# Modulation steps that end 24 steps before the end of layer 0's FFN, and sums of squares on VectorE from the fifth output tile on

## The chip, the core and the metric

The kernel runs on one core of a Trainium2 chip. TensorE multiplies matrices, VectorE and ScalarE work on rows of 128 partitions, GpSimd does so too, SyncE issues DMAs. Each engine works off its own queue of instructions in program order and waits on semaphores for the others. The metric is the device time of one execution in microseconds, as the median of several runs. All times below are microseconds unless marked ns.

## The reference

Four layers in fp32 on 256 tokens of width 1024. The first two (the "first block") have a token mixer and a swiglu FFN, each between two norms, with gates, scales and shifts that come from a modulation vector; in layer 0 a second stream of 256 context tokens goes through the same weights, so that N is 512 there and 256 in layer 1.

```python
mod  = silu(c)     @ w_mod[l] + b_mod[l]      # 6 vectors of 1024 for each layer
modc = silu(c_ctx) @ w_mod[l] + b_mod[l]      # the same for the context stream
h  = rms_norm(xl, g_pre_mix[l]) * (1.0 + sc1) + sh1
y  = token_mixer(h, ...)
xl = xl + gt1 * rms_norm(y, g_post_mix[l])
h  = rms_norm(xl, g_pre_ffn[l]) * (1.0 + sc2) + sh2
xl = xl + gt2 * rms_norm(swiglu(h, ...), g_post_ffn[l])
...                                           # two hybrid layers, and a final norm
```

The change touches the order of `mod` of layer 1 and the end of layer 0, and the sums that the `rms_norm` of y needs.

## The kernel before

Each fp32 matmul is made as three matmuls on split operands (`mm3`, lines 164 to 166): high by high, high by low, low by high. A weight tile arrives by DMA as `raw`; ScalarE rounds it into `whi` (L154), and VectorE, or for some tiles GpSimd, subtracts to get `wlo` (L155). `whi` and `wlo` have four buffers each, `raw` has two. Activations lie transposed, with the model's 1024 channels in eight tiles of 128 partitions and the tokens along the free dimension.

The order of the work is a list of steps with a cost each, written by the planner code below and issued in that order; every engine's queue follows it, with some steps marked as urgent (`soon`) so that they are moved ahead of others. `merge(main, side)` spreads the steps of `side` among those of `main` in proportion to cost, so that both lists end together.

In layer 0's FFN the main list `fs` has 100 steps: gate and up projections and down-projection in two halves of the hidden width. At its end the down-projection's output tiles m=4 to 7 run by halves of the tokens: first half, `y_rms` of the first half and eight `join` tiles (residual, norm, next layer's input), with the second half's tiles between. L1179 adds the two hidden halves on VectorE. The side list `ms` has 71 steps: modulation groups made on VectorE (`mod_v`: L476 and L478, on 512-column `mraw` tiles of w_mod, four parts per group), each group closed by a flush (L484 on TensorE sums over partitions, L489 on VectorE adds the bias).

`y_add` takes an output tile m: ScalarE scales by the gate (`z`, L580), then three sums are built up over m = 0 to 7: the square of y (L596, ScalarE), z*x (L598, VectorE) and the square of z (L599, ScalarE). Tile 0 starts the accumulators `acc`, tile 7 is kept apart as `last`, and L594 adds tiles 1 to 6 in, on GpSimd, only m=6 on VectorE. `y_rms` lets TensorE sum over partitions: L611 reads `acc`, L612 reads `last`; VectorE reads the result (L614, L617), computes the root (lines 269 to 279), TensorE spreads it over the partitions (L316), and VectorE and GpSimd apply it (L645, L646). The next norm makes the input of the next matmuls, tile by tile: L558 on VectorE, L560 on ScalarE, L561 on VectorE.

`y_add` with three sums runs in mixer 0, FFN 0 and mixer 1, and with one sum in FFN 1; where N is 512 the last tiles and `y_rms` go by token halves.

Of the kernel before, what the change touches and what calls it, by code (L numbers as in the profile page):

```python
# [10 lines left out]
ALU = mybir.AluOpType  # L11
# [34 lines left out]
class Kern:  # L46
# [523 lines left out]
    def y_add(self, m, ps, tok, full):  # L570


        nc, V = self.nc, self.v
        t0, t1 = tok
        z = V["z", m]
        G = V["G"]
        x = self.xs[m]
        for s in range(t0 // 256, t1 // 256):
            c = slice(256 * s, 256 * s + 256)
            nc.scalar.activation(z[:, c], ps[:, c], AF.Copy, scale=G[:, m, s:s + 1])  # L580
        c = slice(t0, t1)

        def put(i, f):
            if m == 0:
                V["acc", i] = self.slot()
                f(V["acc", i])
                return
            t = self.slot()
            f(t)
            if m == 7:  # L590
                V["last", i] = t
                return
            a = V["acc", i][:, c]
            (nc.vector if m == 6 else nc.gpsimd).tensor_tensor(a, a, t[:, c], op=ALU.add)  # L594

        put(0, lambda o: nc.scalar.activation(o[:, c], ps[:, c], AF.Square))  # L596
        if full:
            put(1, lambda o: nc.vector.tensor_tensor(o[:, c], z[:, c], x[:, c], op=ALU.mult))  # L598
            put(2, lambda o: nc.scalar.activation(o[:, c], z[:, c], AF.Square))  # L599
# [485 lines left out]
    def block1(self):  # L1085
        nc, a = self.nc, self.a
# [39 lines left out]
        def join(l, N, t0, s_scale, s_shift, gain, hot):  # L1126

            def tile_(i):
                if i == 0:
                    V["pre"] = pre(l, N, t0, s_scale, s_shift, gain)  # L1130
                V["pre"](i, V["rb"][:, 256:], t0 + 256)
            return [H(lambda: self.y_rms(t0, True))] + [X(self.soon(lambda i=i: tile_(i), AHEAD if hot else 0))
                                                        for i in range(8)]

        H = lambda f, c=0.5: ("x", c, self.soon(f))
        for l in range(2):
            N = 512 if l == 0 else 256
            if l == 0:
                fs = [self.mod(0, g) for g in (2, 3, 0, 1)]
                st.append(X(fs[0]))  # L1140
                st.append(X(x_in))
                st += [X(f) for f in fs[1:]]
                st.append(H(pre0))
                st.append(X(self.setup_rest))

            def begin(l, s_gate, gain):
                V["G"] = self.post_cols(l, s_gate, self.par[gain, l])
                for m in range(8):
                    V["z", m] = None

            def y_evac(m, ps, tok):
                if V["z", m] is None:
                    V["z", m] = self.slot()
                self.y_add(m, ps, tok, True)

            jm = lambda t0, hot, l=l, N=N: join(l, N, t0, 4, 3, "g_pre_ffn", hot)
            mix = self.mixer1(l, lambda: self.h, N, y_evac, jm(0, False) if l == 0 else None)
            at = next(i for i in range(len(mix)) if mix[i][0] == "begin")
            mix[at] = X(lambda l=l: begin(l, 2, "g_post_mix"))
            if l == 1:  # L1160
                mix = merge(mix[:8], jf(256, False), 1) + mix[8:]
            P_ = lambda p: st.append(X(lambda: setattr(self, "phase", p), 0))
            P_(2 * l)
            st += mix
            P_(2 * l + 1)
            if l == 1:
                st += self.mem_kv(0)
            st += jm(256 if l == 0 else 0, True)

            def f_evac(m, ps, tok, h, nh, l=l, N=N):  # L1170
                c = slice(*tok)
                if h < nh - 1:
                    V["y", m] = self.slot()
                    nc.scalar.activation(V["y", m][:, c], ps[:, c], AF.Copy)
                    return
                src = ps
                if nh > 1:
                    src = V["y", m]
                    nc.vector.tensor_tensor(src[:, c], src[:, c], ps[:, c], op=ALU.add)  # L1179
                if V["z", m] is None:  # L1180
                    V["z", m] = self.slot()
                self.y_add(m, src, tok, l == 0)

            fs = []
            jf = lambda t0, hot: join(1, 512, t0, 1, 0, "g_pre_mix", hot)
            self.ffn(fs, a["w_ffn_in"][l], a["w_ffn_out"][l], lambda: self.h, N, f_evac,
                     mid=jf(0, False) if l == 0 else None)
            if l == 0:
                ms = []
                self.mod_v(ms, 0, (10, 11), 2)  # L1190
                ms.append(X(lambda: begin(0, 5, "g_post_ffn")))
                self.mod_v(ms, 1, (2, 3, 0, 1), 2)
                self.mod_v(ms, 1, (4, 5, 8, 9, 6, 7, 10, 11), 1)
                fs = merge(fs, ms)
            else:
                fs = merge(fs, [X(self.tables), X(lambda: self.mem_norm(1)), X(lambda: begin(1, 5, "g_post_ffn"))])
            st += fs
            if l == 1:
                st += self.mem_kv(1)
            if l == 1:  # L1200
                def last():
                    self.y_rms(0, False)
                    self.next_h("l0_norm_mix_2")

                    for i in range(8):
                        self.residual(i, 0)
                        self.x_split(i)
                        self.sq_add("x", self.xs[i][:, :256], 256, i, 8)
                st.append(H(last))
# [579 lines left out]
def merge(main, side, now=0):  # L1789

    if now:
        return side[:now] + merge(main, side[now:])
    tot = sum(e[1] for e in main) or 1.0
    ts = sum(max(e[1], 0.05) for e in side) or 1.0
    out = []
    at, done, j = 0.0, 0.0, 0
    for e in main:
        while j < len(side) and done / ts <= at / tot and at > 0:
            out.append(side[j])
            done += max(side[j][1], 0.05)  # L1800
            j += 1
        out.append(e)
        at += e[1]
    return out + side[j:]
# [114 lines left out]
```

## Time and profile before

| quantity | value |
|---|---|
| runs | 2310.51, 2314.38, 2311.95 us; median 2311.95 |
| the profiled execution's own time | 2310.39 us |
| its span | 2308.5 us |
| TensorE busy | 2175.2 us (94%) |
| VectorE busy | 1622.4 us (70%) |
| ScalarE busy | 1085.5 us (47%) |
| GpSimd busy | 535.8 us (23%) |
| L594 on GpSimd | 68 instructions, 70.7 us busy |
| L478 on VectorE | 224 instructions, 174.2 us busy |
| DMA | 319.18 MB, mean 138 GB/s |

The span is the time from the first to the last instruction in the profile; the time of the execution contains it and a little around it. Shares of busy time are averages over stages that differ: TensorE is full in most of the kernel, and waits where one stage ends and the next begins. In the profile PE is TensorE, DVE is VectorE, ACT is ScalarE, POOL is GpSimd; L594 is line 594 of the kernel before. PEclk is the TensorE clock that was granted, as a share of 2.4 GHz.

### The profile page before, as it was taken

To read this page: it belongs to the slowest core of one execution; us is meant where nothing else is said; L and a number is where in the kernel's file an instruction comes from. 1 tells how busy PE (TensorE), PEld (TensorE's weight loads), DVE (VectorE), ACT (ScalarE), POOL (GpSimd) and SP (SyncE) were. 2 spreads that over 40 slices of the span, in tenths; PEclk is the share of its full clock that TensorE was granted. 3 is DMA by queue.
4 is the path that set the end of the run, shared out by engine and by line. 5 is a ranking of instruction groups with operands and counts; after the bars stand their busy time and mean duration, and the time that the engine had idled before them with its cause. 6 is when DMAs were issued, how large, how long until landed. Compare 5 with 4: busy or idle time off the path is not lost.

```text
span 2308.5 us, 37343 instructions
## 1 busy us (share of the span) xinstructions
PE 2175.2 (94%) x14512; PEld 1974.4 (86%) x14512; DVE 1622.4 (70%) x3227; ACT 1085.5 (47%) x2098; POOL 535.8 (23%) x545
## 2 busy tenths in 40 slices
PE   4999999999989999989999999999988999999998
PEld 3777777788888888878888899899976999998998
DVE  5677787959678745577977976775575766676665
ACT  5345665332333222233566555554546544466443
POOL 1354443320340111142333312100343100110000
PEclk8999999999999999998999999999997999999999
DMA  8321112435414555553322455465541555543553
GB/s 276 94 74 55 56 56 74 147 114 173 155 65 155 162 193 165 166 162 115 128 74 74 147 168 184 133 201 172 166 108 58 165 183 174 191 161 100 185 182 120
DMA packets 296625, 319.18 MB, mean 138 GB/s; under 512 B 20544, under 2 KB 264352, under 8 KB 296448
## 3 DMA queue, kind: packets, MB, share of 16 engines
q1 hardware_dynamic: 293072, 311.27, 41.9%
q0 software_dynamic: 2224, 3.43, 0.6%
q8 instruction: 114, 1.87, 0.3%
q10 hardware_dynamic: 1152, 2.10, 0.3%
q14 instruction: 63, 0.52, 0.1%
HBM read 315.72 MB, written 1.05 MB: 137 GB/s over the span
## 4 chain that ended last, share of the span: by engine, by line
PE 73%; DVE 15%; ACT 4%; issue 3%; POOL 2%; DMA 1%; ACTq 0%; DVEq 0%; POOLq 0%
PE p L164 21%; PE p L165 21%; PE p L166 20%; DVE wlo L155 3%; PE p L743 1%; DVE t L478 1%; DVE t L796 1%; PE tr L883 1%; PE p L247 1%; PE p L249 1%; PE p L248 1%; PE tr L484 1%; DVE b L855 1%; PE tr L1267 1%; POOL t L794 1%
## 5 line engine op out<-in xcount | busy, mean ns | idle before, releaser
L164 PE MATMUL p<-t,whi 128*128 128x256 f32 (+1 forms) x3724 | 1176.3, 320 | 10.8 <-ACT t L560 6.5
L166 PE MATMUL p<-t,wlo 128*128 128x256 f32 (+1 forms) x3724 | 1177.4, 317 | 8.9 <-POOL wlo L155 4.7
L165 PE MATMUL p<-t,whi 128*128 128x256 f32 (+1 forms) x3724 | 1179.7, 318 | 3.7 <-DVE t L261 1.7
L164 PEld LDWEIGHTS p<-t,whi 128*128 128x128 f32 x3724 | 716.2, 194 | 60.8 <-ACT t L560 7.8
L166 PEld LDWEIGHTS p<-t,wlo 128*128 128x128 f32 x3724 | 721.1, 194 | 53.5 <-DVE wlo L155 5.5
L165 PEld LDWEIGHTS p<-t,whi 128*128 128x128 f32 x3724 | 722.0, 194 | 47.7 <-DVE t L261 2.5
L154 ACT ACTIVATE whi<-raw 128x1024 fp32r<-128x1024 f32 (+4 forms) x487 | 491.1, 1019 | 502.2 <-PE p L165 302.2
L155 DVE TENSOR_TENSOR wlo<-raw,whi 128x1024 fp32r<-128x1024 f32 (+4 forms) x443 | 549.6, 1242 | 197.0 <-PE p L166 88.3
L155 POOL TENSOR_TENSOR wlo<-raw,whi 128x1024 fp32r<-128x1024 f32 (+2 forms) x44 | 102.9, 2339 | 501.6 <-ACT whi L154 445.1
L478 DVE SCALAR_TENSOR_TENSOR t<-mraw,big,t 128x512 f32<-128x512 f32 x224 | 174.2, 817 | 19.3 <-DMA mraw<-in_w_mod_dram 17.9
L794 POOL TENSOR_TENSOR t<-t,t 128x512 f32<-128x512 f32 (+1 forms) x120 | 136.2, 1135 | 193.3 <-ACT t L793 191.1
L260 ACT ACTIVATE t<-t 128x256 fp32r<-128x256 f32 (+1 forms) x115 | 54.4, 474 | 156.3 <-DVE t L689 112.1
L594 POOL TENSOR_TENSOR t<-t,t 128x256 f32<-128x256 f32 (+1 forms) x68 | 70.7, 1068 | 244.2 <-ACT t L596 240.0
L299 POOL TENSOR_TENSOR t<-t,t 128x256 f32<-128x256 f32 (+1 forms) x27 | 27.1, 1003 | 414.1 <-ACT t L297 403.1
L247 PE MATMUL p<-whi,t 128*128 128x256 f32 x352 | 102.6, 291 | 2.7 <-ACT t L858 2.7
L796 DVE SCALAR_TENSOR_TENSOR t<-u,big,t 128x512 f32<-128x512 f32 (+1 forms) x120 | 102.2, 851 | 0.8
L743 PE MATMUL p<-t,t 64*128 64x256 f32 (+2 forms) x528 | 77.6, 377 | 25.7 <-DVE t L261 11.7
L249 PE MATMUL p<-whi,t 128*128 128x256 f32 x352 | 99.9, 284 | 0.0
L248 PE MATMUL p<-wlo,t 128*128 128x256 f32 x352 | 99.8, 284 | 0.0
L689 DVE TENSOR_TENSOR t<-t,p 128x256 f32<-128x256 f32 (+1 forms) x91 | 43.2, 475 | 78.9 <-PE p L166 78.9
L743 PEld LDWEIGHTS p<-t,t 64*128 64x128 f32 x528 | 50.6, 210 | 46.9 <-issue 18.3
L257 ACT ACTIVATE t<-p 128x256 fp32r<-128x256 f32 x72 | 27.7, 384 | 123.0 <-DVE p L726 98.5
(298 smaller groups left out, 2532.1 us busy)
## 6 DMA issues: line engine op xcount, KB each, us to landing
raw<-in_w_in_dram SPq DMA_DIRECT2D x60, 1024.0 KB, 5.1
raw<-in_l_w_gate_up_dram SPq DMA_DIRECT2D x44, 1024.0 KB, 5.1
raw<-in_w_ffn_in_dram SPq DMA_DIRECT2D x42, 1024.0 KB, 5.2
mraw<-in_w_mod_dram SPq DMA_DIRECT2D x80, 512.0 KB, 4.2
raw<-in_l_w_in_dram SPq DMA_DIRECT2D x15, 1024.0 KB, 5.1
raw<-in_l_w_down_dram SPq DMA_DIRECT2D x16, 896.0 KB, 4.8
t<-in_w_mod_dram SPq DMA_DIRECT2D x32, 256.0 KB, 5.4
raw<-in_w_attn_out_dram SPq DMA_DIRECT2D x8, 1024.0 KB, 5.2
```

The lines of the kernel that those rows point to most:

```text
L154: nc.scalar.activation(p.hi, src, AF.Copy)
L155: eng.tensor_tensor(p.lo, src, p.hi, op=ALU.subtract)
L164: mm(ps, lh, rh, start=first, stop=False)
L165: mm(ps, lh, rl, start=False, stop=False)
L166: mm(ps, ll, rh, start=False, stop=last)
L247: mm(ps[:, :256], lh, p.hi[:, k % 4], start=k == 0, stop=False)
L248: mm(ps[:, :256], lh, p.lo[:, k % 4], start=False, stop=False)
L249: mm(ps[:, :256], ll, p.hi[:, k % 4], start=False, stop=k == 7)
L478: nc.vector.scalar_tensor_tensor(acc, w[:, k], c, acc, op0=ALU.mult, op1=ALU.add)
L743: self.nc.tensor.matmul(out[half], q[i // 2][h, qs], k[i % 2][h, ks], start=i == 0, stop=i == 2)
L794: nc.gpsimd.tensor_tensor(acc, acc, t, op=ALU.add)
L796: i = nc.vector.scalar_tensor_tensor(acc, u, w, acc, op0=ALU.mult, op1=ALU.add)
```

## The change

Two places are edited. In `y_add` the adds of tiles 4 and 5 go to VectorE, as that of tile 6 did. In layer 0 the modulation list is merged with the FFN's steps except the last 24, which follow without any modulation between them. Those 24 are the last seven down-projection steps of the first token half (m=5 to 7), `y_rms` of the first token half, the second halves and the eight `join` tiles.

```diff
@@ -591,7 +591,7 @@
             a = V["acc", i][:, c]
-            (nc.vector if m == 6 else nc.gpsimd).tensor_tensor(a, a, t[:, c], op=ALU.add)
+            (nc.vector if m >= 4 else nc.gpsimd).tensor_tensor(a, a, t[:, c], op=ALU.add)
@@ -1191,7 +1191,9 @@
                 self.mod_v(ms, 1, (2, 3, 0, 1), 2)
                 self.mod_v(ms, 1, (4, 5, 8, 9, 6, 7, 10, 11), 1)
-                fs = merge(fs, ms)
+
+                n = len(fs) - 24
+                fs = merge(fs[:n], ms) + fs[n:]
```

VectorE's queue in FFN 0 around the output tiles m=2 and 3, before (the L598 of m=2 reads t85, that of m=3 t87; x2 is two instructions in a row):

```order
L478 SCALAR_TENSOR_TENSOR t1526_8529<-mraw1533_8579,big_70,t1526_8529 128x512 x2
L155 TENSOR_TENSOR wlo1531_8557<-raw_657,whi1530_8556 128x768
L478 SCALAR_TENSOR_TENSOR t1526_8529<-mraw1540_8615,big_70,t1526_8529 128x512 x2
L478 SCALAR_TENSOR_TENSOR t1526_8529<-mraw1554_8705,big_70,t1526_8529 128x512
L155 TENSOR_TENSOR wlo1535_8584<-raw_657,whi1534_8583 128x768
L478 SCALAR_TENSOR_TENSOR t1526_8529<-mraw1554_8705,big_70,t1526_8529 128x512
L1179 TENSOR_TENSOR t1318_7282<-t1318_7282,p1529_8536 128x512
L598 TENSOR_TENSOR t1538_8609<-t1536_8603,t85_292 128x512
L1179 TENSOR_TENSOR t1322_7310<-t1322_7310,p1532_8560 128x512
L155 TENSOR_TENSOR wlo1548_8653<-raw_657,whi1547_8652 128x640
L598 TENSOR_TENSOR t1545_8646<-t1543_8640,t87_299 128x512
```

The same place after the change:

```order
L598 TENSOR_TENSOR t1531_8549<-t1529_8543,t83_285 128x512
L155 TENSOR_TENSOR wlo1539_8588<-raw_657,whi1538_8587 128x768
L155 TENSOR_TENSOR wlo1542_8611<-raw_657,whi1541_8610 128x768
L1179 TENSOR_TENSOR t1321_7305<-t1321_7305,p1536_8563 128x512
L489 TENSOR_TENSOR big_70<-tr1547_8642,big_70 128x4
L598 TENSOR_TENSOR t1545_8636<-t1543_8630,t85_292 128x512
L1179 TENSOR_TENSOR t1325_7333<-t1325_7333,p1540_8591 128x512
L155 TENSOR_TENSOR wlo1556_8686<-raw_657,whi1555_8685 128x640
L598 TENSOR_TENSOR t1553_8679<-t1551_8673,t87_299 128x512
L489 TENSOR_TENSOR big_70<-tr1558_8708,big_70 128x4
```

Six L478 stood ahead of the L1179 of m=2; none stands between the L598 of m=1 (t83) and that of m=3 now.

VectorE's queue where the first token half ends, from the L598 of m=5 (t91) to that of m=6 (t93) and the adds behind it, before:

```order
L598 TENSOR_TENSOR t1565_8766<-t1563_8761,t91_313 128x256
L476 TENSOR_SCALAR t1571_8797<-mraw1570_8795,big_70 128x512
L478 SCALAR_TENSOR_TENSOR t1571_8797<-mraw1570_8795,big_70,t1571_8797 128x512
L478 SCALAR_TENSOR_TENSOR t1571_8797<-mraw1587_8884,big_70,t1571_8797 128x512
L155 TENSOR_TENSOR wlo1573_8802<-raw_657,whi1572_8801 128x768
L478 SCALAR_TENSOR_TENSOR t1571_8797<-mraw1587_8884,big_70,t1571_8797 128x512
L155 TENSOR_TENSOR wlo1576_8825<-raw_657,whi1575_8824 128x768
L1179 TENSOR_TENSOR t1350_7511<-t1350_7511,p1569_8776 128x256
L478 SCALAR_TENSOR_TENSOR t1571_8797<-mraw1621_9038,big_70,t1571_8797 128x512
L598 TENSOR_TENSOR t1579_8849<-t1577_8844,t93_320 128x256
L594 TENSOR_TENSOR t1516_8488<-t1516_8488,t1578_8846 128x256
L594 TENSOR_TENSOR t1517_8490<-t1517_8490,t1579_8849 128x256
```

The same place after:

```order
L598 TENSOR_TENSOR t1572_8795<-t1570_8790,t91_313 128x256
L594 TENSOR_TENSOR t1524_8516<-t1524_8516,t1571_8792 128x256
L594 TENSOR_TENSOR t1525_8518<-t1525_8518,t1572_8795 128x256
L594 TENSOR_TENSOR t1526_8520<-t1526_8520,t1573_8798 128x256
L155 TENSOR_TENSOR wlo1578_8826<-raw_657,whi1577_8825 128x768
L155 TENSOR_TENSOR wlo1581_8849<-raw_657,whi1580_8848 128x768
L1179 TENSOR_TENSOR t1354_7524<-t1354_7524,p1576_8805 128x256
L598 TENSOR_TENSOR t1584_8873<-t1582_8868,t93_320 128x256
L594 TENSOR_TENSOR t1524_8516<-t1524_8516,t1583_8870 128x256
L594 TENSOR_TENSOR t1525_8518<-t1525_8518,t1584_8873 128x256
L594 TENSOR_TENSOR t1526_8520<-t1526_8520,t1585_8876 128x256
L1179 TENSOR_TENSOR t1357_7546<-t1357_7546,p1579_8829 128x256
```

The L476 and four L478 of the last modulation group are gone from here, and three L594 of m=5 have come in; those of m=4 stand just ahead of the rows.

GpSimd's queue there, from the 512-wide adds of m=3 on, before (t1516 to t1518 are the three accumulators; a wlo is a share of a weight tile):

```order
L594 TENSOR_TENSOR t1516_8488<-t1516_8488,t1544_8643 128x512
L594 TENSOR_TENSOR t1517_8490<-t1517_8490,t1545_8646 128x512
L594 TENSOR_TENSOR t1518_8492<-t1518_8492,t1546_8649 128x512
L155 TENSOR_TENSOR wlo1562_8742<-raw_657,whi1561_8741 128x640
L594 TENSOR_TENSOR t1516_8488<-t1516_8488,t1558_8731 128x256
L594 TENSOR_TENSOR t1517_8490<-t1517_8490,t1559_8734 128x256
L594 TENSOR_TENSOR t1518_8492<-t1518_8492,t1560_8737 128x256
L594 TENSOR_TENSOR t1516_8488<-t1516_8488,t1564_8763 128x256
L594 TENSOR_TENSOR t1518_8492<-t1518_8492,t1566_8769 128x256
L594 TENSOR_TENSOR t1517_8490<-t1517_8490,t1565_8766 128x256
L155 TENSOR_TENSOR wlo1582_8857<-raw_657,whi1581_8856 128x640
L155 TENSOR_TENSOR wlo1630_9082<-raw_657,whi1629_9081 128x640
```

After, with t1524 to t1526 as the accumulators:

```order
L594 TENSOR_TENSOR t1524_8516<-t1524_8516,t1552_8676 128x512
L594 TENSOR_TENSOR t1525_8518<-t1525_8518,t1553_8679 128x512
L594 TENSOR_TENSOR t1526_8520<-t1526_8520,t1554_8682 128x512
L155 TENSOR_TENSOR wlo1569_8771<-raw_657,whi1568_8770 128x640
L155 TENSOR_TENSOR wlo1587_8881<-raw_657,whi1586_8880 128x640
L646 TENSOR_TENSOR t83_285<-t83_285,t1529_8543 128x256
```

The six 128x256 adds of m=4 and 5 are gone; those of 512 columns and the wlo behind them stand as they did.

In all, 32 of the 68 adds on GpSimd move to VectorE: 12 in mixer 0, 12 in FFN 0, 6 in mixer 1 and 2 in FFN 1. The rest of the order differs only in layer 0's FFN, where the modulation steps stand closer together, and slightly among the matmuls at the end of mixer 0, whose adds move.

## Rows read from the trace of the kernel before

**Rows 1.** Windows: start and end, length, busy time and instructions per engine, PEclk, DMA.
```profile
690.00:1000.00 310.00, 310.00 (x1502) 261.64 (x1501) 193.88 (x280) 85.75 (x122) 33.83 (x15) 1.00 0.53 168
1020.00:1040.00 20.00, 12.59 (x97) 11.97 (x96) 18.85 (x23) 8.56 (x17) 17.60 (x12) 0.94 0.57 172
1060.00:1113.00 53.00, 46.81 (x331) 45.43 (x330) 44.97 (x121) 23.99 (x46) 19.27 (x28) 0.87 0.37 119
```

**Rows 2.** Waits of TensorE, 1000 to 1060 us: us in total, times, longest.
```profile
PE tr L611 <- DVE t L594: 4.7, 1, 4.7
PE p L166 <- POOL wlo L155: 1.7, 1, 1.7
PE p L166 <- DVE wlo L155: 1.0, 1, 1.0
```

**Rows 3.** Timeline of TensorE: start, us, then idle before and releaser in brackets.
```profile
1039.04 0.58 PE L611 MATMUL tr<-big,t 128*128 128x1 f32 x2 [4.65 <-DVE t L594]
```

**Rows 4.** Timeline of GpSimd, 1016 to 1036 us.
```profile
1016.66 10.22 POOL L594 TENSOR_TENSOR t<-t,t 128x512 f32<-128x512 f32 x6 [4.34 <-ACT t L596]
1026.85 2.11 POOL L155 TENSOR_TENSOR wlo<-raw,whi 128x640 fp32r<-128x640 f32 x1
1028.92 6.63 POOL L594 TENSOR_TENSOR t<-t,t 128x256 f32<-128x256 f32 x6
```

**Rows 5.** Window of the instructions of L478 alone, VectorE.
```profile
1028.00:1056.00 28.00, 7.36 (x7) 0.76 0.47 142
```

**Rows 6.** Timeline of VectorE, 1028 to 1056 us.
```profile
1036.29 0.41 DVE L1179 TENSOR_TENSOR t<-t,p 128x256 f32<-128x256 f32 x1
1036.62 1.69 DVE L478 SCALAR_TENSOR_TENSOR t<-mraw,big,t 128x512 f32<-128x512 f32 x1
...
1038.57 1.08 DVE L594 TENSOR_TENSOR t<-t,t 128x256 f32<-128x256 f32 x3
...
1047.98 0.16 DVE L614 TENSOR_SCALAR c<-tr 128x2 f32<-128x2 f32 x1 [6.26 <-PE tr L612]
...
1048.32 0.75 DVE L478 SCALAR_TENSOR_TENSOR t<-mraw,big,t 128x512 f32<-128x512 f32 x1
...
1055.23 0.74 DVE L478 SCALAR_TENSOR_TENSOR t<-mraw,big,t 128x512 f32<-128x512 f32 x1
```

**Rows 7.** Windows read for their granted clock (PEclk).
```profile
1039.00:1048.00 9.00, 8.96 (x42) 8.96 (x43) 2.74 (x7) 3.43 (x6) 0.00 (x0) 0.50 0.46 150
1050.00:1052.00 2.00, 2.00 (x14) 2.00 (x13) 0.88 (x5) 0.00 (x0) 0.00 (x0) 0.68 0.00 0
628.00:638.00 10.00, 10.00 (x72) 9.80 (x71) 5.79 (x26) 2.74 (x7) 3.01 (x2) 0.83 0.01 2
```

**Rows 8.** Timeline of VectorE, two wlo beside and without GpSimd's adds.
```profile
1032.34 1.49 DVE L155 TENSOR_TENSOR wlo<-raw,whi 128x768 fp32r<-128x768 f32 x1
...
1058.74 0.82 DVE L155 TENSOR_TENSOR wlo<-raw,whi 128x640 fp32r<-128x640 f32 x1
```

**Rows 9.** Timeline of VectorE, second half of FFN 0.
```profile
1073.13 0.95 DVE L598 TENSOR_TENSOR t<-t,t 128x256 f32<-128x256 f32 x1
...
1075.59 0.97 DVE L598 TENSOR_TENSOR t<-t,t 128x256 f32<-128x256 f32 x1
...
1081.10 0.41 DVE L598 TENSOR_TENSOR t<-t,t 128x256 f32<-128x256 f32 x1
1081.43 1.09 DVE L594 TENSOR_TENSOR t<-t,t 128x256 f32<-128x256 f32 x3
```

**Rows 10.** Line L594 on VectorE: duration ns min/median/max.
```profile
L594 DVE TENSOR_TENSOR t<-t,t x16: 409/414/957, 625.0 to 1648.8; 128x256 f32<-128x256 f32 x16
```

**Rows 11.** Timeline of VectorE: L614 of mixer 0 (second half) and mixer 1.
```profile
668.26 0.16 DVE L614 TENSOR_SCALAR c<-tr 128x2 f32<-128x2 f32 x1 [3.53 <-PE tr L612]
...
1441.06 0.16 DVE L614 TENSOR_SCALAR c<-tr 128x2 f32<-128x2 f32 x1 [2.79 <-PE tr L612]
```

**Rows 12.** Timeline of ScalarE, the split of a weight tile.
```profile
1034.90 0.74 ACT L154 ACTIVATE whi<-raw 128x640 fp32r<-128x640 f32 x1 [4.48 <-DMA raw<-in_w_ffn_out_dram]
```


## The prediction

> **What bounds the kernel now.** I read the windows by stage first, then TensorE's waits, then the timelines of the three engines on either side of the longest wait, and last the granted clock. The windows show where there is something to win. From 690 to 1000 us, in the FFN of layer 0, TensorE is busy all 310.00 us at clock 1.00: whatever VectorE does there beside its 193.88 us is hidden. From 1020 to 1040, where the first token half of the down-projection ends, TensorE has 12.59 of 20 us while VectorE has 18.85 and GpSimd 17.60; from 1060 to 1113, the second half, TensorE has 46.81 of 53 [rows 1]. The waits of 1000 to 1060 name three releasers: the GpSimd wlo (1.7), a VectorE wlo (1.0) and the sum of squares that L611 reads (4.7) [rows 2]; the last stands before the L611 of 1039.04 as 4.65 [rows 3].
>
> The timelines say why. On GpSimd six 512-wide adds take 10.22 us, and the wlo that TensorE waits for stands behind them and takes 2.11 [rows 4]. They start only at 1016.66, after m=2 was summed up late: six L478 stand ahead of its L1179 in VectorE's queue. The six adds of m=4 and 5 then take 6.63 [rows 4]. VectorE between the L598 of m=5 and the last L594 of m=6 works without a gap, and L478 is a large part of it: 7 instructions with 7.36 us from 1028 to 1056 [rows 5], one of which (1.69) stands between the L1179 and the L598 of m=6; the L594 that releases TensorE follows at 1038.57 [rows 6]. So TensorE waits for a VectorE that does modulation work, and for a GpSimd that adds.
>
> The wait costs twice. After it the granted clock is 0.50 from 1039 to 1048, with TensorE busy 8.96 of 9 us, and 0.68 in 1050 to 1052, that is, full again from about 1051.3 [rows 7]: these are the 1.2 and the 2.4 GHz level. VectorE's next step, L614, meanwhile idles 6.26 us for TensorE's L612 [rows 6].
>
> **Part 1, the merge.** The last 24 steps of the FFN list lose one modulation group with its two flushes: the L476 and the seven L478 above, with their four mraw transfers of 512 KB, stand before them now, spread over the stretch that has TensorE full. The GpSimd order shows the six 512-wide adds still ahead of a wlo, but m=2's L1179 no longer behind six L478.
>
> Term 1, the waits. 4.65 + 1.74 + 1.02 = 7.41 us would go [rows 2, 3]. What is late next is the chain of m=7: L1179 (0.41), one wlo (0.82) that the new order has ahead of L598, then L598 (0.41) [rows 6, 8, 9]; TensorE has one L164 and sixteen matmuls to cover it, so I leave one wlo of 0.8 us as a remainder. -6.6. Bounds: -7.4 with none, -5.1 if two wlo, one of them dear (0.82 + 1.49 = 2.3) [rows 8], stand in the way.
>
> Term 2, the clock. From 1039.0 to 1051.3 some 12.3 us ran at half speed; at full speed the same work takes half, a gain of 6.1 at most. A dip will stay: in mixer 0, whose y_rms has no such wait, the clock is 0.83 from 628 to 638 [rows 7], that is 10 x 0.17 x 2 = 3.4 us at half, a loss of 1.7. Upper end 6.1 - 1.7 = 4.4. The 9 us from 1039 to 1048 lie on the path, since VectorE's L614 waits for them; after 1048 VectorE's root is the path and TensorE fills in. So 4.5 - 1.7 = 2.8. Bounds 0 (the dip comes back with the first y_rms) and -4.4. I take -2.8.
>
> Term 3, the root. Two L478 of 0.75 and 0.74 stand between L614 and the residuals, where each instruction waits for the one before [rows 6]. -1.5; 0 if they sat in gaps, -3 if the flush and its wait go with them.
>
> Term 4, denser modulation in the rest of the FFN: some 8.4 us more VectorE work over 310 us in which it has 116 free and TensorE never waited [rows 1]. 0; at most +2 if the mraw transfers push a weight back.
>
> **Part 2, the adds.** 32 of the 68 GpSimd adds go to VectorE: 12 in mixer 0, 12 in FFN 0, 6 in mixer 1, 2 in FFN 1. Alone, three of them take 1.09 us on VectorE, 0.36 each [rows 9]; the extremes are 0.409 and 0.957 for one [rows 10]. In the first halves of mixer 0 and FFN 0 the room is there (term 1 counts the rest). In mixer 1 VectorE idles 2.79 us before L614, more than the six adds' 2.2 [rows 11]; 0, and FFN 1's two likewise.
>
> Term 5, the second half of FFN 0. There TensorE waits for h tiles, which VectorE, ScalarE and VectorE make in turn, and six adds more stand in VectorE's queue: 6 x 0.36 = +2.2. But the two L598 beside GpSimd's adds take 0.95 and 0.97 where the one without takes 0.41 [rows 9]; with GpSimd idle 1.1 comes back. +1.1. Bounds: 0 (hidden in the ScalarE turns) and 6 x 0.957 = +5.7.
>
> The Trainium skill's page "Perfetto Trace Analysis" (Optimizing Scalar/DVE Operations) warns that GpSimd and VectorE share an SBUF port, so that moving work between the two might not help, and "SBUF — State Buffer" (SBUF: two separate sides) calls that port an exclusive lock. The lengthened L598 agree. Were each of the six adds to give back one such wait (0.54), term 5 would be 2.2 - 3.2 = -1.0, and the forecast 2.1 us lower; the trace shows only two lengthened there, so I stay with +1.1.
>
> Term 6, the second half of mixer 0: again six adds, 2.2; VectorE idles 3.53 us before L614 there [rows 11], so most is covered. +0.5, from -1 to +2.2.
>
> **The sum.** -6.6 - 2.8 - 1.5 + 0 + 1.1 + 0.5 = -9.3 us. Against the profiled execution's own 2310.39 us this is 2301.1; that execution is 1.6 below the median of the runs, and the forecast for a median is 2311.95 - 9.3 = 2302.7. Its own range is 2296 to 2307.
>
> **Rivals.** A: the weight stream takes the place of the wait. For it: ScalarE's L154 at 1034.90 had idled 4.48 us for the raw transfer [rows 12], so that TensorE, three microseconds earlier, might meet an unfinished tile. Against it: that transfer waits for a free raw buffer, which VectorE's queue held up too. Price: 4.48 come back and the clock gains nothing: -6.6 + 4.5 - 1.5 + 1.6 = -2.0, 2309.9. Chance 0.20.
>
> B, slower: VectorE becomes what TensorE waits for. 18 of the moved adds stand before a wait of TensorE: 6 ahead of L611 in FFN 0, and 12 among the h tiles of the two second halves. At the dearest row, 0.957, and with no relief they cost 17.2; terms 1 and 3 hold: +17.2 - 6.6 - 1.5 = +9.1, 2321.1. It is slower by a measurable amount once an add costs (6.6 + 1.5 + 4.6) / 18 = 0.71 us. For it: the 0.957, and VectorE's 18.85 of 20. Against it: that row stands beside GpSimd's adds, which are what goes. Chance 0.09.
>
> That the change does nothing is excluded: the order shows the L478 gone from their place and the adds on VectorE.
>
> **The numbers.** Forecast 0.71, A 0.20, B 0.09. A measurement of this kernel tells from no change what exceeds about 0.2%, 4.6 us: faster is below 2307.3. The forecast lies there but for its upper tail, A and that tail are within, B is above: 0.70, 0.21, 0.09. Range: from 2295, all terms near their good ends, to 2310.5, which takes in A.
>
> **What would show it.** Right: TensorE's wait before the first L611 of FFN 0 under 1 us, no wait for a GpSimd wlo from 1000 to 1040, the clock at half for under 5 us after it, L614 to the first residual some 1.5 us shorter. Term 5: TensorE's busy time in the second half unchanged to a microsecond, with L598 at 0.41. Wrong: a new L164 or L166 wait for wlo or whi of a down-projection tile (A), VectorE without idle time from the residuals to the last h tile and TensorE waiting longer there (B), or 690 to 1000 with TensorE below 310.

## The result, and the profile after

The changed kernel takes 2300.08 us in the median of five runs (2297.53 to 2304.33), against 2311.95: the ratio is 0.9948, with a 95% interval of 0.9935 to 0.9961, or 11.9 us less. Forecast were 2302.7, with 2295 to 2310.5. The profiled execution's span is 2297.9 us, 10.6 less than that of before.

The windows of the changed kernel that answer to [rows 1] (start and end, length, then busy time of TensorE, its weight loads, VectorE, ScalarE and GpSimd, the granted clock, DMA):

```profile
690.00:1000.00 310.00, 310.00 (x1518) 262.39 (x1518) 204.47 (x298) 83.53 (x116) 32.39 (x15) 1.00 0.56 178
1020.00:1040.00 20.00, 16.95 (x142) 16.75 (x142) 16.73 (x25) 10.66 (x22) 9.17 (x6) 1.00 0.47 145
1060.00:1113.00 53.00, 48.13 (x314) 44.55 (x313) 45.16 (x116) 24.58 (x47) 11.66 (x20) 0.90 0.39 125
```

The FFN's long stretch is still full at 310.00, with VectorE 10.6 us busier there. From 1020 to 1040 TensorE has 16.95 where it had 12.59, and GpSimd 9.17 where it had 17.60. TensorE's waits from 1000 to 1060, as in [rows 2]:

```profile
PE tr L611 <- DVE t L594: 3.1, 1, 3.1
PE tr L316 <- DVE c L279: 0.7, 1, 0.7
```

Both waits of L166 for a wlo are gone, that for the sums is not: it is 3.05 long, in the timeline that answers to [rows 3]:

```profile
1038.67 0.38 PE L611 MATMUL tr<-big,t 128*128 128x1 f32 x2 [3.05 <-DVE t L594]
```

Why, three queues tell. GpSimd makes the six adds of m=2 and 3 in three pieces now, as the tiles come, and its wlo is ready before TensorE needs it; compare [rows 4]:

```profile
1016.82 3.81 POOL L594 TENSOR_TENSOR t<-t,t 128x512 f32<-128x512 f32 x3 [0.60 <-ACT t L596]
1021.11 1.35 POOL L594 TENSOR_TENSOR t<-t,t 128x512 f32<-128x512 f32 x1 [0.48 <-ACT t L596]
1023.16 3.93 POOL L594 TENSOR_TENSOR t<-t,t 128x512 f32<-128x512 f32 x2 [0.69 <-DVE big L489]
1027.04 1.77 POOL L155 TENSOR_TENSOR wlo<-raw,whi 128x640 fp32r<-128x640 f32 x1
```

VectorE holds no modulation work there any more (against [rows 6]), and yet stands idle 2.51 us before the L598 of m=6, since it waits for ScalarE's L580:

```profile
1033.83 0.42 DVE L1179 TENSOR_TENSOR t<-t,p 128x256 f32<-128x256 f32 x1
1036.76 1.52 DVE L598 TENSOR_TENSOR t<-t,t 128x256 f32<-128x256 f32 x1 [2.51 <-ACT t L580]
1038.20 1.08 DVE L594 TENSOR_TENSOR t<-t,t 128x256 f32<-128x256 f32 x3
1039.21 0.41 DVE L1179 TENSOR_TENSOR t<-t,p 128x256 f32<-128x256 f32 x1
1039.54 0.81 DVE L155 TENSOR_TENSOR wlo<-raw,whi 128x640 fp32r<-128x640 f32 x1
1040.27 0.42 DVE L598 TENSOR_TENSOR t<-t,t 128x256 f32<-128x256 f32 x1
1043.58 0.16 DVE L614 TENSOR_SCALAR c<-tr 128x2 f32<-128x2 f32 x1 [2.89 <-PE tr L612]
```

And ScalarE could have begun that L580 at about 1034.2, when the L1179 of m=6 was done. It stood behind a L154, the split of a weight tile for later, that waited for TensorE to be done with a buffer:

```profile
1035.59 0.74 ACT L154 ACTIVATE whi<-raw 128x640 fp32r<-128x640 f32 x1 [2.80 <-PE p L166]
1036.23 0.49 ACT L580 ACTIVATE t<-t,c 128x256 f32<-128x256 f32 x1
```

TensorE released it with the last L166 that it ran ahead of the wait, and then waited for the sums: ScalarE's queue had them behind work that TensorE did not need yet. The same L154 let GpSimd start its share of that weight tile, and beside it the L598 of m=6 took 1.52 us (above) where it takes 0.41 otherwise:

```profile
1036.45 1.54 POOL L155 TENSOR_TENSOR wlo<-raw,whi 128x640 fp32r<-128x640 f32 x1 [7.64 <-ACT whi L154]
```

So of the 3.05 us of waiting some 2.0 are the late L580 (1036.23, not 1034.2), and some 1.1 the long L598.

The windows that answer to [rows 7] show that the clock is still full in the wait and behind it, and falls only from 1043.5 to 1047.5; mixer 0's dip of 628 to 638 is the same as before:

```profile
1036.00:1040.00 4.00, 1.33 (x11) 1.33 (x12) 3.24 (x6) 2.31 (x6) 1.54 (x1) 1.00 0.41 137
1043.50:1047.50 4.00, 4.00 (x23) 4.00 (x23) 3.62 (x23) 0.54 (x1) 0.00 (x0) 0.57 0.05 17
628.00:638.00 10.00, 9.98 (x71) 9.61 (x70) 4.38 (x26) 1.87 (x6) 0.00 (x0) 0.83 0.01 2
```

The stages are cut at VectorE's L614, with which the root begins, and at the six L645 that end it. Of the changed kernel:

```profile
679.62 2.08 DVE L645 TENSOR_TENSOR t<-t,tr 128x256 f32<-128x256 f32 x6 [0.68 <-PE tr L316]
...
1048.37 0.75 DVE L645 TENSOR_TENSOR t<-t,tr 128x256 f32<-128x256 f32 x2 [0.16 <-PE tr L316]
...
1054.94 2.08 DVE L645 TENSOR_TENSOR t<-t,tr 128x256 f32<-128x256 f32 x6 [0.68 <-PE tr L316]
```

with 1043.58 for the first L614, above. The stretch from mixer 0's six L645 to that L614, in one window, before

```profile
676.89:1047.98 371.09, 361.75 (x1827) 310.22 (x1826) 244.36 (x352) 111.86 (x172) 64.94 (x39) 0.98 0.52 164
```

and after:

```profile
679.62:1043.58 363.96, 358.37 (x1835) 307.08 (x1834) 241.33 (x362) 111.15 (x171) 56.84 (x33) 1.00 0.52 167
```

TensorE's busy time fell by 3.4 us with nearly the same number of matmuls (the clock), and the time it was not busy from 9.3 to 5.6 (the waits).

The second half of FFN 0, to be held against [rows 9], has L598 at 0.41 and the adds at 1.08 for three:

```profile
1064.55 0.41 DVE L598 TENSOR_TENSOR t<-t,t 128x256 f32<-128x256 f32 x1
1064.88 1.08 DVE L594 TENSOR_TENSOR t<-t,t 128x256 f32<-128x256 f32 x3
...
1067.81 0.41 DVE L598 TENSOR_TENSOR t<-t,t 128x256 f32<-128x256 f32 x1
```

The whole stretch, from the first six L645 of FFN 0 to the second six, before and after:

```profile
1062.91:1099.95 37.04, 32.90 (x229) 31.73 (x228) 29.59 (x79) 15.39 (x27) 14.29 (x14) 0.86 0.39 125
1054.94:1092.94 38.00, 35.01 (x243) 33.59 (x242) 31.00 (x86) 16.53 (x28) 9.75 (x8) 0.87 0.43 138
```

It holds 14 matmuls more than before, and TensorE is busy 2.1 us longer in it; the time that it was not busy fell from 4.1 to 3.0, mostly by one wait for a GpSimd wlo, 2.9 before and 1.1 after.

All adds of line 594 on VectorE (compare [rows 10]; ns, minimum, median, maximum), and the two L614 of [rows 11]:

```profile
L594 DVE TENSOR_TENSOR t<-t,t x48: 409/416/1797, 622.6 to 1638.4; 128x256 f32<-128x256 f32 x48
```

```profile
672.55 0.16 DVE L614 TENSOR_SCALAR c<-tr 128x2 f32<-128x2 f32 x1 [3.74 <-PE tr L612]
...
1432.04 0.16 DVE L614 TENSOR_SCALAR c<-tr 128x2 f32<-128x2 f32 x1 [3.35 <-PE tr L612]
```

The dearest add now takes 1.797 us, but the median is where it was; the idle time ahead of L614 in the mixers has not shrunk, so the moved adds were covered there.

### The profile page after: what moved, and what is told of

The parts are those of the page before. It is cut to its first block, busy times and chain, and to the rows that moved or that the text cites. A ratio compares the mean times of both kernels' runs of the same rounds, so it can differ in the third digit from the quotient of the medians.

```text
span 2297.9 us, 37350 instructions
## 1 busy us (share of the span) xinstructions
PE 2172.5 (95%) x14512; PEld 1970.2 (86%) x14512; DVE 1622.3 (71%) x3259; ACT 1083.9 (47%) x2098; POOL 508.1 (22%) x513
## 4 chain that ended last, share of the span: by engine, by line
PE 71%; DVE 16%; ACT 5%; issue 4%; DMA 2%; POOL 1%; ACTq 0%; DVEq 0%; POOLq 0%; SPq 0%
PE p L164 20%; PE p L165 20%; PE p L166 20%; DVE wlo L155 3%; DVE t L796 1%; PE p L743 1%; DVE t L478 1%; PE p L247 1%; PE p L249 1%; PE tr L883 1%; PE p L248 1%; DVE b L855 1%; PE tr L484 1%; DVE t L258 1%; ACT whi L154 1%
## 5 line engine op out<-in xcount | busy, mean ns | idle before, releaser
L166 PE MATMUL p<-t,wlo 128*128 128x256 f32 (+1 forms) x3724 | 1176.6, 317 | 2.9 <-DVE wlo L155 1.6
L166 PEld LDWEIGHTS p<-t,wlo 128*128 128x128 f32 x3724 | 718.7, 193 | 47.9 <-DVE wlo L155 3.2
L154 ACT ACTIVATE whi<-raw 128x1024 fp32r<-128x1024 f32 (+4 forms) x487 | 491.8, 1020 | 522.9 <-PE p L165 341.5
L478 DVE SCALAR_TENSOR_TENSOR t<-mraw,big,t 128x512 f32<-128x512 f32 x224 | 166.6, 782 | 24.7 <-DMA mraw<-in_w_mod_dram 23.4
L299 POOL TENSOR_TENSOR t<-t,t 128x256 f32<-128x256 f32 (+1 forms) x27 | 27.1, 1002 | 413.3 <-ACT t L297 412.8
L594 POOL TENSOR_TENSOR t<-t,t 128x256 f32<-128x256 f32 (+1 forms) x36 | 40.5, 1153 | 220.6 <-ACT t L596 217.3
```

Of the source, the lines that this page charges most:

```text
L154: nc.scalar.activation(p.hi, src, AF.Copy)
L166: mm(ps, ll, rh, start=False, stop=last)
L478: nc.vector.scalar_tensor_tensor(acc, w[:, k], c, acc, op0=ALU.mult, op1=ALU.add)
```

## The experiments

All were timed against the kernel before, run beside them on the same chip; ratios are given with their 95% intervals.

**The merge alone.** The adds as before, the modulation 24 steps early:

```diff
-            (nc.vector if m >= 4 else nc.gpsimd).tensor_tensor(...)
+            (nc.vector if m == 6 else nc.gpsimd).tensor_tensor(...)
```

> The modulation steps end 24 steps early; the adds stay as before (only m=6 on VectorE). Theory 'modulation' (the wait at FFN 0's end was VectorE's modulation work): nearly all of the gain is here, 2300 to 2303 us; TensorE's waits from 1000 to 1060 fall from 8.5 to 2 to 4 us, half clock after the first L611 for under 5 us. Rival 'GpSimd' (the wlo and the sums behind GpSimd's slow adds hold TensorE up): only about half, 2305 to 2308 us, with a wait of L166 for a GpSimd wlo or of L611 for an add that GpSimd's chain delays.

Measured: 2305.71 us, 0.9971 [0.9960, 0.9983], some 6.7 us less than before: by the time this is in the range of rival 'GpSimd'. The waits are as theory 'modulation' had them. Its first L611 waits no longer than that of the changed kernel:

```profile
PE tr L611 <- DVE t L594: 2.3, 1, 2.3
```

GpSimd's six adds still take 6.43 us there, but end at 1033.0, ahead of the adds of m=6 at 1035.3, so they hold no sum up:

```profile
1026.61 6.43 POOL L594 TENSOR_TENSOR t<-t,t 128x256 f32<-128x256 f32 x6
```

ScalarE's split tile blocks here too, this time for a transfer:

```profile
1032.73 0.74 ACT L154 ACTIVATE whi<-raw 128x640 fp32r<-128x640 f32 x1 [2.82 <-DMA raw<-in_w_ffn_out_dram]
```

So the adds are not why TensorE waits, but the rest of the gain is missing, and half speed lasts longer than the 5 us that the theory allowed: neither theory holds whole. In the stage up to L614 TensorE is not busy for 5.7 us, as in the changed kernel (5.6); it is busy 2.2 us longer, mostly from the clock, shown for the 25 us around the first L614, in this kernel and in the changed one:

```profile
1028.72:1053.72 25.00, 22.72 (x151) 22.35 (x149) 16.05 (x50) 8.65 (x16) 8.24 (x8) 0.80 0.40 126
```

```profile
1028.58:1053.58 25.00, 21.85 (x170) 21.44 (x168) 19.10 (x59) 10.18 (x20) 4.15 (x4) 0.93 0.45 143
```

25 x 0.20 x 2 = 10 us at half speed against 25 x 0.07 x 2 = 3.5.

**The mixers' adds alone.** The merge as before, the adds of m=4 and 5 on VectorE in the mixers:

```diff
+            (nc.vector if (m >= 4 if self.phase in (0, 2) else m == 6) else nc.gpsimd).tensor_tensor(...)
...
+                fs = merge(fs, ms)
```

> The merge as before; the adds of m=4 and 5 on VectorE in the two mixers alone. Theory 'modulation': 2311.5 to 2313.5 us (mixer 0's second half +0.5, mixer 1 nothing). Rival 'GpSimd': 2307 to 2310 us, since GpSimd's adds slow VectorE beside them; the 2.0 us that the changed kernel gained between 1100 and 1441 us would be seen here too.

2312.68 us, 0.9996 [0.9985, 1.0006]: these 18 adds give nothing, as theory 'modulation' said. The FFN's adds without the new merge were not tried.

**First halves only.** Tiles 4 and 5 on VectorE only where the tokens begin at 0:

```diff
+            (nc.vector if (m >= 4 if t0 == 0 else m == 6) else nc.gpsimd).tensor_tensor(...)
```

> As the changed kernel, but m=4 and 5 go to VectorE only where the token range begins at 0; the second halves of mixer 0 and FFN 0 add on GpSimd as before. Theory 'modulation', with term 5 of +1.1 and term 6 of +0.5: 1.5 us faster than the changed kernel, 2298 to 2299.5 us, and the stretch from the six L645 of FFN 0's first half to those of the second about 37.0 us where the changed kernel has 38.0. Rival 'GpSimd': the same as the changed kernel or up to 2 us slower, that stretch not shorter.

2302.36 us, 0.9952 [0.9941, 0.9964], not faster than the changed kernel: the expectation for the time fell. The stretch from FFN 0's first six L645 to the second six was 37.2 us against the changed kernel's 38.0, as expected; mixer 0's second half (34.1 against 32.8) and the FFN after it (365.9 against 364.0) lost more than that. The next run shows that such differences are within the scatter.

**The changed kernel again.**

> The changed kernel once more, unedited, to see how far one profiled execution's stages repeat. Theory 'repeats': 2299 to 2301.5 us, and each stage (from one y_rms to the next) within 1 us of the first profile; then the 2.0 us gained between 1100 and 1441 are the change's. Rival 'spread': the median agrees, but the stages that the change leaves alone differ by 2 us or more from one profile to the next; then those 2.0 us are no effect.

2301.39 us, 0.9953 [0.9935, 0.9971]. The first stage differs by 2.5 us between the two profiles (the first L614 at 634.52 and 632.03), one in mixer 0 by 2.1, the others by at most 1.1, and layer 1 took 339.10 and 339.02 us. The kernels that leave layer 1 alone or not took 340 to 346 there, with no order in it. So rival 'spread' holds: a stage of one execution can be read to some 2 to 2.5 us, and the 2.0 us that layer 1 seemed to gain are not shown to be the change's.

**The FFN's adds, and the mixers'.** Three kernels with the new merge: adds of m=4 and 5 on VectorE in the FFNs only, in the mixers only, and in layer 0 only.

```diff
+            (nc.vector if (m >= 4 if self.phase == 1 else m == 6) else nc.gpsimd).tensor_tensor(...)
...
+            (nc.vector if (m >= 4 if self.phase in (0, 2) else m == 6) else nc.gpsimd).tensor_tensor(...)
...
+            (nc.vector if (m >= 4 if self.phase < 2 else m == 6) else nc.gpsimd).tensor_tensor(...)
```

> As the changed kernel, but the adds of m=4 and 5 go to VectorE only in the FFNs, in the mixers they stay on GpSimd. Theory 'FFN 0' (what the adds give beyond the merge, 5 us, is won at FFN 0's end): 2299.5 to 2302 us. Rival 'everywhere' (12 adds in mixer 0 and 6 in mixer 1 carry their share): 2302.5 to 2305 us, half way to the kernel with the merge alone.

> Modulation ends 24 steps early and the adds of m=4 and 5 go to VectorE in the mixers alone; FFN 0 adds as before. So far the merge alone gave -6.6, the merge with the FFN's adds -5.9 to -6.7, both with all adds -11, the mixers' adds without the merge nothing. Theory 'mixers after the merge' (the mixers' adds carry the other 5): 2299.5 to 2302.5 us. Rival 'both needed': 2303.5 to 2306 us, no better than the merge alone, so that only all adds together shorten the half clock at FFN 0's end.

> Modulation ends 24 steps early, adds of m=4 and 5 on VectorE in mixer 0 and FFN 0, in layer 1 as before. Theory 'layer 0': 2299.5 to 2302 us, the changed kernel's time, since mixer 1's six adds had room before. Rival 'mixer 1': 2303 to 2306 us, layer 1's mixer 2 us longer than the 339 of the changed kernel.

| kernel, all with the new merge | median us | ratio | mixer 0, first to second six L645 | from there to FFN 0's L614 |
|---|---|---|---|---|
| no add moved | 2305.71 | 0.9971 [0.9960, 0.9983] | 33.9 | 366.3 |
| FFNs only | 2306.48 | 0.9971 [0.9960, 0.9982] | 34.0 | 367.0 |
| first halves only | 2302.36 | 0.9952 [0.9941, 0.9964] | 34.1 | 365.9 |
| mixers only | 2302.81 | 0.9965 [0.9950, 0.9980] | 32.2 | 363.1 |
| layer 0 only | 2300.36 | 0.9953 [0.9938, 0.9967] | 32.8 | 363.8 |
| all, the change | 2300.08 | 0.9948 [0.9935, 0.9961] | 32.8 | 364.0 |
| all, again | 2301.39 | 0.9953 [0.9935, 0.9971] | 35.3 | 365.1 |

The FFN's adds give nothing by themselves (2306.48 is beyond 'FFN 0' and its rival), layer 1's give nothing ('layer 0' holds). 'Mixers only' ends between its two theories. The two columns of stages go by whether mixer 0's second half adds on VectorE: 395 to 397 us together where it does, and once 400; 400 to 401 where it does not. The medians of 'mixers only' and 'layer 0 only' lie 2.4 us apart with intervals that overlap, so whether both are needed is not settled.

**Modulation up to 8 steps before the end.**

```diff
-                n = len(fs) - 24
+                n = len(fs) - 8
```

> As the changed kernel, but the modulation ends 8 steps before the end, not 24: three L478 stand again between the L598 of m=5 and that of m=6, none behind L614. Theory 'queue' (terms 1 and 2, the waits and the clock behind them, carry the merge's gain): most of it is lost, 2306 to 2311 us, L611's wait back at 4 us or more. Rival 'root' (term 3, the L478 between L614 and the residuals, carries it): 2300 to 2303 us, L614 to the first residual about 4.8 us as in the changed kernel, L611's wait not the point.

2308.65 us, 0.9985 [0.9972, 0.9997]: two thirds of the gain are gone, as theory 'queue' said. No L478 stands behind L614, which is 6.4 us ahead of the first residual (4.8 in the changed kernel, 8.7 before), but three stand ahead of the adds of m=6, and the wait is back:

```profile
PE tr L611 <- DVE t L594: 5.5, 1, 5.5
PE p L166 <- DVE wlo L155: 1.8, 3, 0.9
```

A flush does stand behind L614, after the root and ahead of the residuals:

```profile
1048.37 0.16 DVE L489 TENSOR_TENSOR big<-tr,big 128x4 f32<-128x4 f32 x1 [1.01 <-PE tr L484]
```

The profile is of an execution of 2303.41 us, the fastest of the twelve.

**m=6 on VectorE.** Scaling and both squares of m=6, first token half of FFN 0:

```diff
+            if hot:
+                nc.vector.tensor_scalar(z[:, c], ps[:, c], G[:, m, s:s + 1], None, op0=ALU.mult)
+            else:
+                nc.scalar.activation(z[:, c], ps[:, c], AF.Copy, scale=G[:, m, s:s + 1])
...
+        sq = lambda o, x_: nc.vector.tensor_tensor(o, x_, x_, op=ALU.mult) if hot else nc.scalar.activation(o, x_, AF.Square)
...
+                self.y_add(m, src, tok, l == 0, l == 0 and m == 6 and tok[0] == 0)
```

> As the changed kernel; for m=6, first token half of FFN 0, the scaling and both squares are made on VectorE, not ScalarE. In the changed kernel TensorE still waits 3.05 us at the first L611 there. Theory 'queue of ScalarE' (the L580 of m=6 stands behind an L154 that waits 2.80 us for a weight buffer): the wait falls to about 1.3 us and the time by 1.5 to 2, 2298 to 2299 us. Rival 'VectorE's adds' (the three adds and VectorE's queue set it): wait 2.5 to 4 us, time unchanged to 1 us longer, 2300 to 2301.

2298.25 us, 0.9934 [0.9921, 0.9947], the best of all; the interval overlaps the changed kernel's. TensorE's wait at L611 is gone, wholly, in the profiled execution, which took 2291.45 us and is the fastest of the five by some 3.5. The longest waits from 1000 to 1060 come later, in the root (1046.42) and in the second half (1056.61, where the changed kernel has 1.13 us for the same wlo); line numbers are 3 to 5 higher in this kernel:

```profile
PE p L166 <- POOL wlo L155: 1.5, 1, 1.5
PE tr L316 <- DVE c L279: 1.1, 1, 1.1
```

VectorE runs from the L1179 of m=6 (here L1183) to the adds without waiting:

```profile
1028.16 0.41 DVE L1183 TENSOR_TENSOR t<-t,p 128x256 f32<-128x256 f32 x1
1028.61 0.35 DVE L581 TENSOR_SCALAR t<-t,c 128x256 f32<-128x256 f32 x1
1028.88 0.42 DVE L599 TENSOR_TENSOR t<-t 128x256 f32<-128x256 f32 x1
1029.21 0.42 DVE L602 TENSOR_TENSOR t<-t,t 128x256 f32<-128x256 f32 x1
1029.55 0.75 DVE L597 TENSOR_TENSOR t<-t,t 128x256 f32<-128x256 f32 x2
```

That shows that ScalarE's queue held the sums up, not the adds; the long L598 is gone with it (L602 takes 0.42 here), so the two are not told apart. The stage up to L614 is 361.6 us, 2.4 less than in the changed kernel, about what such a stage scatters. Half speed is still there, some 3.5 us, though TensorE no longer waits at L611:

```profile
1020.56:1045.56 25.00, 24.78 (x193) 24.29 (x191) 20.99 (x62) 11.55 (x22) 6.75 (x5) 0.93 0.51 159
```

**Further along the same way.** On top of that kernel: modulation 48 steps early; m=5 on VectorE as well; all adds from m=2 on VectorE.

```diff
+                n = len(fs) - 48
...
+                self.y_add(m, src, tok, l == 0, l == 0 and m >= 5 and m < 7 and tok[0] == 0)
...
+            (nc.vector if m >= 2 else nc.gpsimd).tensor_tensor(a, a, t[:, c], op=ALU.add)
```

> The kernel with m=6 made on VectorE (FFN 0, first token half), and the modulation ends 48 steps before the end instead of 24. Theory 'done' (with 24 no modulation is left among the last tiles, so ending earlier moves only hidden work): 2297 to 2299.5 us, 690 to 1000 us with TensorE full. Rival 'crowding' (the same 71 steps in fewer steps delay weights): TensorE below 310 in that stretch and 2299.5 to 2303 us.

> As the kernel with m=6 of FFN 0's first half made on VectorE, and m=5 there too. Theory 'queue of ScalarE': m=5's sums were not late (its L580 waited for L1179, not for L154), so nothing is won: 2297.5 to 2300 us, no wait at the first L611. Rival 'more is better': 2295 to 2297. Rival 'VectorE full': a wait for a wlo from VectorE comes in its place, 2300 to 2303.

> The kernel with m=6 made on VectorE, and the adds from m=2 on are VectorE's too, 512 columns wide in FFN 0's tiles 2 and 3. Theory 'GpSimd slows VectorE': its adds make VectorE's instructions beside them twice as long, so taking them away pays: 2294 to 2297.5 us and no wait for a GpSimd wlo near 1040. Rival 'VectorE full': six 512-wide adds of some 0.7 us more in its queue, 2299 to 2303 us, with waits for wlo of VectorE before the first L611.

The first, 2302.59 us, 0.9959 [0.9945, 0.9974], is as 'crowding' had it: at the start of the FFN VectorE has four L478 in a row ahead of a product that TensorE needs,

```profile
PE p L164 <- DVE t L693: 3.4, 1, 3.4
```

and the stage to L614 is 369.6 us. The second, 2299.47, 0.9949 [0.9935, 0.9964], and the third, 2299.02, 0.9948 [0.9931, 0.9964], win nothing over m=6 alone. The wait at the first L611 is none in the third, but 1.54 us in the first and 0.85 in the second, where none was expected: VectorE has no gap ahead of it there, so it is VectorE's own queue that is late. The third misses 'GpSimd slows VectorE' (2294 to 2297.5); by the time it is at the edge of 'VectorE full', whose waits for a wlo of VectorE do not show, and TensorE has its 20.00 of 1020 to 1040.

## Why the prediction was right, and which step of it failed

The direction and the time were right; the split was not, and two errors met. By its terms the merge is worth -10.9 (terms 1 to 4) and the adds cost 1.6 (terms 5 and 6). Measured, the merge alone gives 6.7 us, and the adds together with it another 4 to 5, with intervals that touch or overlap. That the sum is within 3 us is partly luck.

| term | forecast | profile after less before | read from |
|---|---|---|---|
| 1, the waits | -6.6 | -3.7 | TensorE not busy, mixer 0's residuals to FFN 0's L614: 9.3 to 5.6 |
| 2, the clock | -2.8 | -3.4 | TensorE busy in the same stage: 361.75 to 358.37 |
| 3, the root | -1.5 | -3.6 | L614 to the six L645: 14.93 to 11.36 |
| 4, denser modulation | 0 | 0 | 310.00 of 310 in both |
| 5, adds in FFN 0's second half | +1.1 | +1.0 | first to second six L645: 37.04 to 38.00 |
| 6, adds in mixer 0's second half | +0.5 | -1.1 | first to second six L645: 33.87 to 32.75 |
| sum | -9.3 | -10.8 | |

The last column holds for this pair of profiles. In the second profile of the changed kernel the same stages give -7.2 (term 6 is +1.4 there). And the stages outside the table moved by +3.9 ahead of it and -3.6 behind, which cancel by chance.

**Term 1 is the step that failed.** "What is late next is the chain of m=7" was wrong: late next was m=6, whose L580 stood behind a L154 in ScalarE's queue. The wait left over was 3.05 us, not 0.8 and beyond the bound of 2.3. The row that told it was there, in [rows 12]: that L154, idle for 4.48, stood ahead of the L580 of m=6 in the kernel before too. It did not bind there, because L1179 came later still, as the row behind it says:

```profile
1036.79 0.51 ACT L580 ACTIVATE t<-t,c 128x256 f32<-128x256 f32 x1 [1.16 <-DVE t L1179]
```

I read the L154 as rival A, a weight tile late for TensorE; no weight was late, but what is queued behind the tile on ScalarE was. A's mechanism thus came in part, and A's price of 4.5 and its lost clock did not. The experiment with m=6 on VectorE shows it: without ScalarE's part the wait is gone in that profile. The prediction also took 0.41 for the L598 on this path; beside GpSimd's wlo it took 1.52, a lengthening that it had priced only in the second half.

**Term 2** was right in kind: some 12.3 us at half speed became 3.5, about what the prediction let stay. It is no steady gain, as the second profile of the same kernel has 7 us.

**Term 3** was too small because it counted the two L478 alone. L614 to the first L645 lost 3.9 us, and three more rows of the kernel before stand in that chain: a wlo that waits for TensorE, an L1179 that does, and an L279 (0.15 otherwise) beside GpSimd's wlo of 1053.41:

```profile
1051.46 0.96 DVE L155 TENSOR_TENSOR wlo<-raw,whi 128x768 fp32r<-128x768 f32 x1 [1.12 <-PE p L166]
...
1053.22 0.42 DVE L1179 TENSOR_TENSOR t<-t,p 128x256 f32<-128x256 f32 x1 [0.40 <-PE p L166]
1053.55 1.43 DVE L279 SCALAR_TENSOR_TENSOR c<-b,c 128x1 f32<-128x1 f32 x1
```

The two L478, 1.12, 0.40 and 1.28 make about 4.3; waits of 0.26 and 0.16 stand in the changed kernel's chain. TensorE's half speed does not tell the two apart: between L614 and the first L645 it lasts some 3.3 us before (clock 0.81 over 8.66 us) and 3.4 after (0.64 over 4.79). The cut at 8 steps has 6.4 us there, with the flush above in its chain.

**Term 5** came to the forecast number, but not as it was worked out. L598 at 0.41 shows the relief and the adds at 1.08 the cost; the stretch however holds 14 matmuls more, so TensorE's busy time was not "unchanged to a microsecond", and its waits fell. Among the kernels of the table above the stretch takes 37.2 to 37.8 us with these adds on GpSimd and 37.9 to 38.7 with them on VectorE: about 0.8, no more than such a stage scatters. The Trainium skill's page "SBUF — State Buffer" (SBUF: two separate sides) calls the port that GpSimd and VectorE share an exclusive lock; the two L598 that are short again agree with it. The -1.0 that the prediction worked out for six such waits does not show.

**Term 6** had the wrong sign in this pair. Where mixer 0's second half adds on VectorE it takes 32.2 to 33.1 us in eight profiles, against 33.9 to 34.1 in four where it does not; the second profile of the changed kernel has 35.3, with the clock at 0.84 there against 0.93. Idle time before L614 covered the adds. That GpSimd no longer slows what stands beside it may be the gain; no run shows it.

**Rival B** is out: VectorE's adds cost 0.36 each in the second half, and the waits of TensorE for h tiles there (1060 to 1113 us) are 1.7 us in all against 0.9.

Of the signs that the prediction named, no wait for a GpSimd wlo from 1000 to 1040, the half clock under 5 us (in the first profile), 310 of 310 and L598 at 0.41 came; the wait at L611 under 1 us and the unchanged busy time of the second half did not, and L614 to the first residual is 3.9 us shorter, not 1.5.

What stays open: why the half clock after the first L611 lasts 3.5 us in some kernels and 7 or 10 in others. It does not follow the wait: 2.3 us of waiting with 10, 3.05 with 3.5, none with 3.5 (m=6 on VectorE), 1.54 with no half speed at all (48 steps early), and two profiles of the same changed kernel have 3.5 and 7. In the changed kernel, with m=6 on VectorE and in mixer 0 it begins within a microsecond of the last L612, whose matmuls are one column wide; no run varies that. Of the 5 us between the merge alone and the whole change, the profiles show 3.4 from mixer 0's first six L645 to FFN 0's last (2.2 of TensorE's busy time up to L614, 1.2 in mixer 0's second half), described but not explained. The rest lies in stretches that scatter with no order by what was edited: over all profiles 639 to 647 us up to mixer 0's first six L645, and 1205 to 1213 from FFN 0's last to the end.

## What to carry to other kernels

When a wait is to go, follow the chain that releases it through every queue it passes, and ask of each instruction ahead of it what that one waits for: an instruction for later work that waits for a buffer blocks everything queued behind it. Deferrable work ahead of a join can cost more than its own length: before the change, 7.4 us of waits came with 12.3 us at half clock, though how much clock a wait costs did not follow from the wait. And what moves work between engines should be timed in parts: here the sum was forecast well and its parts were not.

## What the runs showed of the hardware

How much half speed TensorE had did not follow from the wait before it. In the kernel before, a wait of 4.65 us was followed by half speed from the first matmuls on [rows 7]; in the changed kernel the clock was 1.00 in a wait of 3.05 us and for some 5 us of matmuls behind it, and 0.57 only from 1043.5 to 1047.5. With m=6 on VectorE some 3.5 us of half speed came without a wait at L611, and with the modulation 48 steps early a wait of 1.54 us had a clock of 1.00 in all the 25 us around it.

VectorE's three adds of m=4 took 2.47 us (at 1027.30), beside GpSimd's wlo of 1027.04 and its 1.77, those of m=5 1.09 (at 1031.09) with GpSimd idle; L598 took 1.52 instead of 0.41 beside GpSimd's wlo of 1036.45. Moved work is slowed by what stays.
